# Recurrence gates of a hybrid encoder block as pairs of 64-row matmuls, with r and i brought together by transfers

## The chip, the cores and the metric

The kernel runs on one core of a Trainium2 chip. The metric is the device time of one execution in microseconds (us), as the median of several runs. The profile of a kernel is one execution recorded by the hardware profiler; its engines are PE (matrix multiply; PEld is its weight load), DVE (vector), ACT (scalar and activation functions), POOL and SP (which issue transfers, POOL also small fills).

## The reference

One layer on a sequence of 512 tokens with 1024 features: a half-step SwiGLU feed-forward block, a mixing stage, a second half-step feed-forward block. The mixing stage projects the normalised input to seven groups of 1024 columns; one of them goes through a short convolution and then through two gated linear recurrences, one forward and one backward in time. Their gates are what the change touches: the 1024 features form 16 blocks of 64, and each block has its own 64x64 weight for each direction and each of the two gates r and i.

```python
def _rglru_scan(xc, w_gates, b_gates, lam):
    xb = xc.reshape(B_, S, LRU_BLOCKS, LRU_BLOCK)
    gates = jnp.einsum('bsni,gnio->gbsno', xb, w_gates).reshape(2, B_, S, W)
    gates = gates + b_gates[:, None, None, :]
    r = jax.nn.sigmoid(gates[0])
    i = jax.nn.sigmoid(gates[1])
    log_a = -LRU_C * r * jax.nn.softplus(-lam)
    a = jnp.exp(log_a)
    bx = jnp.sqrt(-jnp.expm1(2.0 * log_a)) * (i * xc)
    _, h = lax.associative_scan(_lin_combine, (a, bx), axis=1)
    return h
```

## The kernel before

Activations lie with features on the 128 partitions and the 512 tokens along the free dimension: a tile `f` is 128 features (two gate blocks of 64) by 512 tokens, and there are eight tiles. Matmuls are float32 in three parts: an operand is split into a high part H (by ACT, line 118) and a low remainder L (by DVE, line 121), and a product is H·H + H·L + L·H (`mm3`, lines 144 to 147).

The stages in order: first feed-forward block (`ffn`, with the Strassen-like `strassen`, line 260); the projection that feeds the recurrence, eight chunks (the loop at line 641, with `conv` after each); the q, k, v projections in two halves (`tok_group`, lines 656 to 670, called t0 and t1); the three gate projections of the merge (`gates`, line 836, called g); the output projection; the second feed-forward block.

Two generators run beside these stages, the "lanes": `lru` (line 583), once for tiles 0 to 3 and once for tiles 4 to 7 (lane 0 and lane 1 below), and `heads` (line 710), the attention. `weave` (line 449) advances a lane by so many `yield` steps after each chunk; RATE (line 59) says how many. This order in the program is a priority: a planner at build time orders the instructions of each engine, starting what is ready by its own estimate of times. `after(i, prev)` (line 199) forces the order of two instructions without a wait.

In `lru`, for each tile and each direction `d`, each gate `g` gets one group of three 128x128x512 matmuls (lines 603 and 604). The weight is 128x128 with the two 64x64 blocks of the tile on its diagonal and zeros elsewhere. A sigmoid on ACT (line 606) takes the result out of PSUM; `ix` is multiplied by the convolution's result (line 611) and tanh of the scaled r is taken (line 613) at once. After the four tiles come the exponentials (618), the square roots (623) and the scans (631, 633), one step of the lane for each. The last result `A[f]` is used at line 856, in stage g.

Buffers: four PSUM banks named `acc` for the projections and four named `aux` for the lanes; 48 SBUF slots of 2 KB per partition (`big`), among which are r, ix and th; four slots of twice that size (`pair`); three raw and four split weight buffers. Transfers: weights on SP's queue; on POOL's queue the eight stores and six loads that shift V (lines 693 and 696) and the sixteen loads of the attention bias (line 706). POOL also zeroes the padding of the convolution's input (lines 569 and 570).

Of the kernel before, what the change touches and what calls it, by code (L numbers as in the profile page):

```python
# [11 lines left out]
AF = mybir.ActivationFunctionType  # L12
ALU = mybir.AluOpType
# [3 lines left out]
P = 128  # L17
T = 512
D = 1024
KT = D // P  # L20
# [3 lines left out]
HD = 64  # L24
# [10 lines left out]
C_BG = 64  # L35
# [17 lines left out]
GB_BATCH = (range(0, 4), range(4, 6), range(6, 7), range(7, 8))  # L53

LRU_F = 4

ATT_LAG = 1, 2

# [9 lines left out]
def block_kernel(ctx: ExitStack, tc, a, out):  # L68
    nc = tc.nc
# [11 lines left out]
    def nm(s):  # L81
        uid[0] += 1
        return f"{s}_{uid[0]}"
# [3 lines left out]
    def big_t(dt=F32, shape=(P, T), n="b"):  # L87
        return big.tile(list(shape), dt, tag="big", bufs=NBIG, name=nm(n))
# [4 lines left out]
    def acc_t():  # L93
        return acc.tile([P, T], F32, tag="acc", name=nm("acc"))

    def aux_t():
        return aux.tile([P, T], F32, tag="aux", name=nm("aux"))


    small = const.tile([P, NSMALL], F32, name="small")  # L100
# [15 lines left out]
    def split(raw, H, L, act=True):  # L116
        if act:
            nc.scalar.activation(H, raw, AF.Copy)  # L118
        else:
            nc.vector.tensor_copy(H, raw)  # L120
        nc.vector.tensor_tensor(L, raw, H.bitcast(F32), ALU.subtract)  # L121
# [3 lines left out]
    def raw_t():  # L125
        return wpool.tile([P, 1024], F32, tag="wraw", bufs=3, name=nm("wraw"))

    def hl_t():
        return (wpool.tile([P, 1024], F32R, tag="wh", bufs=4, name=nm("wh")),
                wpool.tile([P, 1024], F32R, tag="wl", bufs=4, name=nm("wl")))  # L130

    def load_w(src, n, act=True):
        raw = raw_t()
        H, L = hl_t()
        s = slice(0, n)
        ld = nc.sync.dma_start(raw[:, s], src[:, s])
        if nld[0] < 8:
            tc.keep_in_program_order(ld)
        nld[0] += 1
        with tc.high_priority():  # L140
            split(raw[:, s], H[:, s], L[:, s], act)
        return H, L

    def mm3(ps, wh, wl, xh, xl, first, last):
        nc.tensor.matmul(ps, wh, xh, start=first, stop=False)  # L145
        nc.tensor.matmul(ps, wh, xl, start=False, stop=False)  # L146
        nc.tensor.matmul(ps, wl, xh, start=False, stop=last)  # L147
# [48 lines left out]
        nc.scalar.activation(r, ps, AF.Copy)  # L196
        return r, rcol, vx

    def after(i, prev):

        i, prev = getattr(i, "ins", i), getattr(prev, "ins", prev)
        tc.add_manual_dep(i, prev.name, mybir.DependencyInfo(
            mybir.DependencyClass.NoSync, mybir.DependencyReason.DATA), reason="order")


    mark = {}
# [242 lines left out]
    def weave(rate):  # L449
        for ln, n in rate.items():  # L450
            q = lanes[ln]
            due[ln] += n
            while due[ln] >= 1 and q:
                try:
                    next(q[0])
                    due[ln] -= 1
                except StopIteration:
                    q.pop(0)
            if not q:
                due[ln] = 0.0  # L460
# [86 lines left out]
    sp4 = const.tile([P, 16], F32, name="sp4")  # L547
# [17 lines left out]
    xc = [None] * KT  # L565
# [13 lines left out]


    last_act = [None]

    def lru(fs):
        un = []
        cuts = {}

        def cut(f):
            if f in fs:
                cuts[f] = big_t(F32R, n="ch"), big_t(F32R, n="cl")
                split(xc[f], *cuts[f])  # L590

        cut(fs[0])
        for f in fs:
            gH, gL = load_w(a["wgate"][f], T)
            cut(f + 1)
            cH, cL = cuts.pop(f)
            yield
            for d in range(2):
                rt = []
                for g in range(2):  # L600
                    q = d * 2 + g
                    s = slice(q * P, (q + 1) * P)
                    ps = aux_t()
                    mm3(ps, gH[:, s], gL[:, s], cH, cL, True, True)
                    t = big_t(n="gate")
                    i = nc.scalar.activation(t, ps, AF.Sigmoid, bias=small[:, C_BG + f * 4 + q : C_BG + f * 4 + q + 1])
                    if last_act[0] is not None:
                        after(i, last_act[0])
                    rt.append(t)
                r, ix = rt  # L610
                nc.vector.tensor_tensor(ix, ix, xc[f], ALU.mult)
                th = big_t(n="th")
                tanh = nc.scalar.activation(th, r, AF.Tanh, scale=sp4[:, f * 2 + d : f * 2 + d + 1])
                un.append((f, d, r, ix, th))
                yield

        for f, d, r, ix, th in un:
            exp = nc.scalar.activation(r, r, AF.Exp, scale=sn8[:, f * 2 + d : f * 2 + d + 1])
            after(exp, tanh)
            nc.vector.scalar_tensor_tensor(ix, r, 1.0, ix, ALU.add, ALU.mult)  # L620
            yield
        for f, d, av, ix, th in un:
            last_act[0] = nc.scalar.activation(th, th, AF.Sqrt)
            after(last_act[0], exp)
            nc.vector.tensor_tensor(ix, ix, th, ALU.mult)
            yield
        h = None
        for f, d, av, ix, th in un:
            if d == 0:
                h = th  # L630
                nc.vector.tensor_tensor_scan(h, av, ix, 0.0, ALU.mult, ALU.add)
            else:
                nc.vector.tensor_tensor_scan(th[:, ::-1], av[:, ::-1], ix[:, ::-1], 0.0, ALU.mult, ALU.add)
                nc.vector.tensor_tensor(h, h, th, ALU.add)
                A[f] = h
            yield
# [4 lines left out]
    for f in range(KT):  # L641
        ps = acc_t()
# [234 lines left out]
    for m in range(KT):  # L877
        nc.sync.dma_start(xres[m], xd[m])
        ps = acc_t()
# [21 lines left out]
def layouts(inp):  # L901

    f = lambda n: np.asarray(inp[n])
    con = np.ascontiguousarray
    o = {}
    x = f("x")[0].reshape(ROWS, NCB, QC, KT, P)
    o["x"] = con(x.transpose(3, 4, 1, 0, 2)).reshape(KT, P, T)

    def feat(w):
        k, n = w.shape  # L910
        return con(w.reshape(k // P, P, n // P, P).transpose(2, 1, 0, 3)).reshape(n // P, P, k)

# [12 lines left out]
    o["wg3"] = np.concatenate([feat(w[:, c]) for c in (1, 5, 6)], 0)  # L925
    qkv = w[:, 2:5].reshape(4, 2, P, 3, 2, T)
    o["wqkv"] = con(qkv.transpose(3, 4, 0, 2, 1, 5)).reshape(6, 4, P, 2 * T)
    o["wout"] = feat(f("w_out")[0])
    wg = f("lru_w_gates")[0]
    bd = np.zeros((KT, P, 4, P), wg.dtype)  # L930
    for b in range(16):
        s = slice((b % 2) * 64, (b % 2) * 64 + 64)
        bd[b // 2, s, :, s] = wg[:, :, b].reshape(4, 64, 64).transpose(1, 0, 2)
    o["wgate"] = bd.reshape(KT, P, 4 * P)
    col = lambda v: np.asarray(v).reshape(-1, KT, P).transpose(2, 1, 0).reshape(P, -1)
    o["small"] = con(np.concatenate([
        col(f("norm_ffn1")[0]), col(f("norm_mix")[0]), col(f("norm_ffn2")[0]),
        col(f("conv_w")[0]), col(f("conv_b")[0]),
        col(f("lru_b_gates")[0].reshape(4, D)), col(f("lru_lambda")[0]),
        np.tile(f("q_norm")[0], 2)[:, None], np.tile(f("k_norm")[0], 2)[:, None]], 1))  # L940


    rp = f("rel_pos_bias")[0]
    t = np.full((NH, ROWS, QC, 3, 2, ROWS, QC), -1.0e30, rp.dtype)
    for ty, n in enumerate((0, 1, 3)):
        for p in range(QC):
            c = n * QC + QC - 1 - p
            cs = min(max(c - 8, 0), GW - 16)
            for k in range(cs, cs + 16):
                hf, kc = divmod(k - KSTART[n], QC)  # L950
                for r in range(ROWS):

# [21 lines left out]
```

## Time and profile before

| what | us |
|---|---|
| median of 3 runs | 1135.82 |
| lowest and highest | 1135.45, 1135.82 |
| the profiled execution | 1135.38 |
| its span, first to last instruction | 1133.6 |
| PE busy | 1126.1 (99%) |
| DVE busy | 836.4 (74%) |
| ACT busy | 594.5 (52%) |
| POOL busy | 19.2 (2%) |

Rows of instructions read: start, duration, engine, line of the kernel, operation, output tile <- input tiles, shapes, how many. A matmul's row is longer than its share of PE, because matmuls overlap in the array: the distance between the starts of two neighbours is what one costs. In rows of groups, the numbers behind the bar are the busy time and the mean length of one, and behind the second bar the idle time of the engine before them, with what ended it.

### The profile page before, as it was taken

The page shows a single profiled execution, that of the slowest core. Times are in us where ns is not written, and L with a number is a line of the kernel's source. Part 1 is how long each engine was busy: PE and PEld are TensorE (multiplying, and loading weights), DVE is VectorE, ACT ScalarE, POOL GpSimd, SP SyncE. Part 2 cuts the span into 40 slices and gives each one's busy share as a digit, 9 for nine tenths or more (in the row PEclk, how much of TensorE's full clock was granted, in tenths as well). Part 3 has the DMA queues.
Part 4 walks back from the last instruction along what each step waited for, and adds up shares of the span by engine and source line. Part 5 has one row for each costly group of instructions (what it writes and reads, how often), then busy time and mean ns, then how long its engine had stood idle before and what let it go on. Part 6 is the DMA issues. An engine that isn't in the chain of part 4 may idle for free.

```text
span 1133.6 us, 17247 instructions
## 1 busy us (share of the span) xinstructions
PE 1126.1 (99%) x6872; PEld 994.0 (88%) x6872; DVE 836.4 (74%) x1288; ACT 594.5 (52%) x896; POOL 19.2 (2%) x52
## 2 busy tenths in 40 slices
PE   9999999999999999999999999999999999999998
PEld 7899999988888888888788887888999999998886
DVE  7898888884836798797855576758688888894542
ACT  8554544563624595985564254656445545464330
POOL 0000000000000000010110000000000000000000
PEclk9999999999999999999999999999999999999999
DMA  8242333443333342453453333355134333353420
GB/s 266 89 131 79 123 97 108 132 133 103 121 98 107 97 158 81 119 170 93 135 145 103 93 102 87 109 168 186 56 83 123 94 110 114 90 171 94 130 75 38
DMA packets 43553, 130.69 MB, mean 115 GB/s; under 512 B 5968, under 2 KB 8272, under 8 KB 43472
## 3 DMA queue, kind: packets, MB, share of 16 engines
q1 hardware_dynamic: 39600, 119.36, 34.4%
q0 software_dynamic: 3296, 9.97, 2.9%
q8 instruction: 54, 0.88, 0.3%
q10 hardware_dynamic: 576, 0.26, 0.1%
q14 instruction: 27, 0.22, 0.1%
HBM read 121.17 MB, written 8.39 MB: 114 GB/s over the span
## 4 chain that ended last, share of the span: by engine, by line
PE 96%; DVE 3%; ACT 1%; issue 0%; DMA 0%; ACTq 0%; DVEq 0%
PE acc L260 29%; PE acc L146 11%; PE acc L145 11%; PE acc L147 11%; PE aux L260 5%; PE aux L145 4%; PE aux L146 4%; PE aux L147 4%; PE acc L666 3%; PE acc L665 3%; PE acc L667 3%; PE aux L794 1%; DVE wl L121 1%; PE aux L783 1%; DVE so L767 1%; PE aux L757 1%
## 5 line engine op out<-in xcount | busy, mean ns | idle before, releaser
L118 ACT ACTIVATE wh<-wraw 128x1024 fp32r<-128x1024 f32 (+3 forms) x242 | 241.5, 999 | 334.6 <-PE acc L260 96.8
L121 DVE TENSOR_TENSOR wl<-wraw,wh 128x1024 fp32r<-128x1024 f32 (+3 forms) x254 | 291.7, 1151 | 137.6 <-ACT wh L118 136.9
L260 PE MATMUL acc<-s,wh 128*128 128x256 f32 x1216 | 220.6, 283 | 0.1
L260 PEld LDWEIGHTS acc<-s,wh 128*128 128x128 f32 x1216 | 189.7, 192 | 0.3 <-ACT p L317 0.3
L260 PE MATMUL acc<-s,wl 128*128 128x256 f32 x608 | 172.1, 283 | 0.0
L145 PE MATMUL acc<-xh,wh 128*128 128x512 f32 x304 | 120.3, 396 | 0.0
L146 PE MATMUL acc<-xl,wh 128*128 128x512 f32 x304 | 119.5, 393 | 0.0
L147 PE MATMUL acc<-xh,wl 128*128 128x512 f32 x304 | 119.0, 391 | 0.0
L260 PEld LDWEIGHTS acc<-s,wl 128*128 128x128 f32 x608 | 116.7, 192 | 0.0
L260 PE MATMUL acc<-xh,wl 128*128 128x256 f32 x304 | 86.0, 283 | 0.0
L260 PE MATMUL acc<-xl,wh 128*128 128x256 f32 x304 | 86.0, 283 | 0.0
L260 PE MATMUL acc<-xh,wh 128*128 128x256 f32 x304 | 86.0, 283 | 0.0
L665 PE MATMUL acc<-wh,xh 128*128 128x512 f32 x192 | 75.4, 393 | 0.0
L666 PE MATMUL acc<-wh,xl 128*128 128x512 f32 x192 | 74.8, 390 | 0.0
L667 PE MATMUL acc<-wl,xh 128*128 128x512 f32 x192 | 74.8, 389 | 0.0
L294 DVE TENSOR_TENSOR wraw<-wraw,pair 128x1024 f32<-128x1024 f32 x57 | 69.6, 1221 | 0.8
L145 PE MATMUL aux<-hh,wh 128*128 128x512 f32 x176 | 68.5, 389 | 0.0
L146 PE MATMUL aux<-hl,wh 128*128 128x512 f32 x176 | 68.5, 389 | 0.0
L147 PE MATMUL aux<-hh,wl 128*128 128x512 f32 x176 | 68.5, 389 | 0.0
L145 PE MATMUL acc<-hh,wh 128*128 128x512 f32 x176 | 68.5, 389 | 0.0
L146 PE MATMUL acc<-hl,wh 128*128 128x512 f32 x176 | 68.5, 389 | 0.0
L147 PE MATMUL acc<-hh,wl 128*128 128x512 f32 x176 | 68.5, 389 | 0.0
(194 smaller groups left out, 2197.1 us busy)
## 6 DMA issues: line engine op xcount, KB each, us to landing
wraw<-wqkv SPq DMA_DIRECT2D x24, 512.0 KB, 3.7
wraw<-wg SPq DMA_DIRECT2D x24, 512.0 KB, 3.6
wraw<-w1d SPq DMA_DIRECT2D x22, 512.0 KB, 3.6
wraw<-w2d SPq DMA_DIRECT2D x22, 512.0 KB, 3.6
pair<-w2s SPq DMA_DIRECT2D x20, 512.0 KB, 3.6
wraw<-w2s SPq DMA_DIRECT2D x20, 512.0 KB, 3.7
wraw<-w1s SPq DMA_DIRECT2D x18, 512.0 KB, 3.8
pair<-w1s SPq DMA_DIRECT2D x18, 512.0 KB, 3.7
```

Of the source, the lines that this page charges most:

```text
L118: nc.scalar.activation(H, raw, AF.Copy)
L121: nc.vector.tensor_tensor(L, raw, H.bitcast(F32), ALU.subtract)
L145: nc.tensor.matmul(ps, wh, xh, start=first, stop=False)
L146: nc.tensor.matmul(ps, wh, xl, start=False, stop=False)
L147: nc.tensor.matmul(ps, wl, xh, start=False, stop=last)
L260: nc.tensor.matmul(o, w_[:, c], x_, start=first and m + k == 0 and w_ is H and x_ is xh_, stop=m + k == 4 and w_ is L, skip_group_check=True)
L294: nc.vector.tensor_tensor(t, t, o, ALU.add)
L665: nc.tensor.matmul(pss[j], xh[kk][:, tj], H[:, s], start=kk == 0, stop=False)
L666: nc.tensor.matmul(pss[j], xl[kk][:, tj], H[:, s], start=False, stop=False)
L667: nc.tensor.matmul(pss[j], xh[kk][:, tj], L[:, s], start=False, stop=kk == KT - 1)
L757: nc.tensor.matmul(ps[hp][:, i * 256 : (i + 1) * 256], q_[o, n * P : (n + 1) * P], keys(k_[o]), start=k_ is kh and q_ is qh, stop=q_ is ql)
L767: nc.vector.tensor_tensor_reduce(so[:, cs], ps[hp][:, cs], bm[:, BTYPE[n]], -1.0, 3.0e38, ALU.add, ALU.min, nmx[:, i : i + 1])
```

## The change

- The gate weights are stored without zeros: for each tile 128 partitions (two blocks of 64 rows) by 256 columns, which are, for each direction, 64 columns of r and 64 of i.
- For a tile, all four PSUM banks are taken at once. Each direction has three products (H·H, H·L, L·H), and each product is a pair of matmuls with 64 rows, one for the block on partitions 0 to 63 and one for the block on 64 to 127. That is a run of six pairs per tile, held together by `after`. The first of them waits (with a semaphore, `sync=True`) for the last sigmoid of the tile before.
- A result bank now holds r of one block on partitions 0 to 63 and i of the same block on 64 to 127. The sigmoids, four per tile as before, write them to a `pair` buffer, `both`; four transfers on POOL's queue per direction (64 rows of 2 KB each) put the two r halves into `r` and the two i halves into `ix`.
- The product with `xc` and tanh (`use`) move from directly behind the sigmoids to two tiles later (`LRU_LAG`); a lane has five steps more, 41 instead of 36.
- On the host, the layout of the gate weights and of their bias follows.

```diff
+LRU_LAG = 2
...
-    def after(i, prev):
+    def after(i, prev, sync=False):
...
-            mybir.DependencyClass.NoSync, mybir.DependencyReason.DATA), reason="order")
+            mybir.DependencyClass.Sync if sync else mybir.DependencyClass.NoSync, mybir.DependencyReason.DATA), reason="order")
...
+        def use(f, d, r, ix):
+            nc.vector.tensor_tensor(ix, ix, xc[f], ALU.mult)
+            th = big_t(n="th")
+            un.append((f, d, r, ix, th))
+            return nc.scalar.activation(th, r, AF.Tanh, scale=sp4[:, f * 2 + d : f * 2 + d + 1])
...
-            gH, gL = load_w(a["wgate"][f], T)
+            gH, gL = load_w(a["wgate"][f], 2 * P)
             cut(f + 1)
             cH, cL = cuts.pop(f)
             yield
+            ps = [[aux_t() for _ in range(2)] for _ in range(2)]
+            mm = None
             for d in range(2):
-                rt = []
-                for g in range(2):
-                    q = d * 2 + g
-                    s = slice(q * P, (q + 1) * P)
-                    ps = aux_t()
-                    mm3(ps, gH[:, s], gL[:, s], cH, cL, True, True)
-                    t = big_t(n="gate")
-                    i = nc.scalar.activation(t, ps, AF.Sigmoid, bias=small[:, C_BG + f * 4 + q : C_BG + f * 4 + q + 1])
+                c = slice(d * P, (d + 1) * P)
+                for W, X in ((gH, cH), (gH, cL), (gL, cH)):
+                    for b in range(2):
+                        o = slice(b * HD, (b + 1) * HD)
+                        prev, mm = mm, nc.tensor.matmul(
+                            ps[d][b], W[o, c], X[o], start=W is gH and X is cH, stop=W is gL)
+                        if prev is not None:
+                            after(mm, prev)
+                        elif evicted:
+                            after(mm, evicted[-1], True)
+            for d in range(2):
+                q = C_BG + f * 4 + d * 2
+                both = pair_t()
+                for b in range(2):
+                    i = nc.scalar.activation(both[:, b], ps[d][b], AF.Sigmoid, bias=small[:, q + b : q + b + 1])
                     if last_act[0] is not None:
                         after(i, last_act[0])
-                    rt.append(t)
-                r, ix = rt
-                nc.vector.tensor_tensor(ix, ix, xc[f], ALU.mult)
-                th = big_t(n="th")
-                tanh = nc.scalar.activation(th, r, AF.Tanh, scale=sp4[:, f * 2 + d : f * 2 + d + 1])
-                un.append((f, d, r, ix, th))
-                yield
+                evicted.append(i)
+                r, ix = (big_t(n="gate") for _ in range(2))
+                for g, t in enumerate((r, ix)):
+                    for b in range(2):
+                        nc.gpsimd.dma_start(t[b * HD : (b + 1) * HD], both[g * HD : (g + 1) * HD, b])
+                got.append((f, d, r, ix))
+            yield
+            while len(got) > 2 * LRU_LAG:
+                tanh = use(*got.pop(0))
+            yield
+        for _ in range(LRU_LAG):
+            yield
+            yield
+            for t in got[:2]:
+                tanh = use(*t)
+            got = got[2:]
+        yield
...
-    o["wgate"] = bd.reshape(KT, P, 4 * P)
+    o["wgate"] = con(wg.reshape(2, 2, KT, 2, 64, 64).transpose(2, 3, 4, 0, 1, 5)).reshape(KT, P, 4 * 64)
```

More of the change, by code (lines that the diff above doesn't have):

```diff
@@ L581, in block_kernel @@
     last_act = [None]
+    evicted = []
     def lru(fs):
         un = []
+        got = []
         cuts = {}
+        def use(f, d, r, ix):
[3 more added lines that the diff above has]
+            return nc.scalar.activation(th, r, AF.Tanh, scale=sp4[:, f * 2 + d : f * 2 + d + 1])
         def cut(f):
@@ L929, in layouts @@
     wg = f("lru_w_gates")[0]
[L930 to L933, printed above, removed]
-    o["wgate"] = bd.reshape(KT, P, 4 * P)
+    o["wgate"] = con(wg.reshape(2, 2, KT, 2, 64, 64).transpose(2, 3, 4, 0, 1, 5)).reshape(KT, P, 4 * 64)
     col = lambda v: np.asarray(v).reshape(-1, KT, P).transpose(2, 1, 0).reshape(P, -1)
+    bg = f("lru_b_gates")[0].reshape(2, 2, KT, 2, 64).transpose(1, 4, 2, 0, 3).reshape(P, 4 * KT)
     o["small"] = con(np.concatenate([
@@ L938, in layouts @@
         col(f("conv_w")[0]), col(f("conv_b")[0]),
-        col(f("lru_b_gates")[0].reshape(4, D)), col(f("lru_lambda")[0]),
+        bg, col(f("lru_lambda")[0]),
         np.tile(f("q_norm")[0], 2)[:, None], np.tile(f("k_norm")[0], 2)[:, None]], 1))
```

## The prediction

> **What bounds the kernel now.** I read the page first, its busy times and its chain.
>
> ```profile
> span 1133.6 us, 17247 instructions
> PE 1126.1 (99%) x6872; PEld 994.0 (88%) x6872; DVE 836.4 (74%) x1288; ACT 594.5 (52%) x896; POOL 19.2 (2%) x52
> PE 96%; DVE 3%; ACT 1%; issue 0%; DMA 0%; ACTq 0%; DVEq 0%
> ```
>
> PE carries 96% of the chain that ends last. A busy PE need not be a PE at its peak, so the next view is the timeline of PE at one tile's gates, where what counts is the step from one start to the next, not the length of a row.
>
> ```profile
> 389.87 0.39 PE L147 MATMUL acc<-xh,wl 128*128 128x512 f32 x1
> 390.09 0.39 PE L145 MATMUL aux<-ch,wh 128*128 128x512 f32 x1
> 390.32 0.39 PE L146 MATMUL aux<-cl,wh 128*128 128x512 f32 x1
> ...
> 392.59 0.39 PE L147 MATMUL aux<-ch,wl 128*128 128x512 f32 x1
> 392.81 0.39 PE L145 MATMUL acc<-xh,wh 128*128 128x512 f32 x1
> ```
>
> From 390.09 to 392.81 PE starts this tile's twelve gate matmuls and nothing else: 2.72 us, 0.227 us each, the same as its neighbours. There is no idle to win; the only way to shorten this stage is to give PE less. The question is then whether the other engines can follow. The same stretch by windows, columns as in its first row:
>
> ```profile
> core 0: us, PE busy (x) PEld busy (x) DVE busy (x) ACT busy (x) POOL busy (x), PEclk, DMA share, GB/s
> 400.00:410.00 10.00, 10.00 (x46) 8.25 (x45) 9.26 (x12) 10.00 (x15) 0.92 (x2) 1.00 0.87 295
> 410.00:420.00 10.00, 10.00 (x45) 8.28 (x45) 9.62 (x14) 9.94 (x14) 0.00 (x0) 1.00 0.33 101
> 440.00:450.00 10.00, 10.00 (x46) 8.28 (x45) 6.76 (x12) 2.64 (x4) 0.00 (x0) 1.00 0.26 79
> 480.00:490.00 10.00, 10.00 (x46) 8.29 (x45) 9.12 (x14) 9.97 (x15) 2.27 (x4) 1.00 0.64 189
> ```
>
> ACT is full at 400 to 420 and at 480 to 490, yet PE loses nothing there; between the two bursts ACT has room (2.64 of 10). The waits say why:
>
> ```profile
> ACT wh L118 <- PE acc L666: 33.7, 11, 4.8
> PE aux L783 <- DVE nmx L767: 0.8, 2, 0.6
>   PEld aux L145: 0.4, 1
> ```
>
> The first row (all waits): the weight splits of the q, k, v projections wait 33.7 us for PE to free a buffer, so the splits are ahead of PE. The second is the longest wait of PE itself after the start; the third, from the gates' own tile view, is the only one PE had on a gate sigmoid, 0.4 us.
>
> **The change part by part.**
>
> *Fewer matmul steps.* The gate matmuls between 380 and 490 us, by line:
>
> ```profile
> L145 PE MATMUL aux<-ch,wh 128*128 128x512 f32 x32 | 12.2, 397 | 0.0
> L146 PE MATMUL aux<-cl,wh 128*128 128x512 f32 x32 | 12.5, 389 | 0.0
> L147 PE MATMUL aux<-ch,wl 128*128 128x512 f32 x32 | 12.5, 389 | 0.0
> ```
>
> 96 matmuls at 0.227 us are 21.8 us. Half of each 128x128 weight is zeros. The change makes them 96 matmuls with 64 rows, in pairs on rows 0 to 63 and 64 to 127, each pair with its two results in two banks. The trace has that form already, in the attention scores:
>
> ```profile
> 524.30 0.39 PE L667 MATMUL acc<-wl,xh 128*128 128x512 f32 x1
> 524.62 0.38 PE L757 MATMUL aux<-kh,qh 64*128 64x256 f32 x2
> 524.85 0.28 PE L757 MATMUL aux<-kl,qh 64*128 64x256 f32 x2
> 524.97 0.28 PE L757 MATMUL aux<-kh,ql 64*128 64x256 f32 x2
> ...
> 525.32 0.29 PE L757 MATMUL aux<-kh,ql 64*128 64x256 f32 x2
> 525.54 0.66 PE L731 MATMUL aux<-ident,qk 128*128 128x128 f32 x4
> ...
> 526.39 0.48 PE L665 MATMUL acc<-wh,xh 128*128 128x512 f32 x1
> 526.70 0.39 PE L666 MATMUL acc<-wh,xl 128*128 128x512 f32 x1
> ```
>
> Each row is a pair, and pairs follow at 0.12 us for 256 columns: half of the 0.227 that 512 columns take, for two matmuls. So a pair costs what one matmul costs; for 512 columns I take 0.227. 48 pairs are 10.9 us: 10.9 us less.
>
> *Going in and out of 64 rows.* The same rows price it. Into the run: 524.30 to 524.62 is 0.32 where 0.23 is usual (+0.09); the first pair to the second is 0.23 instead of 0.12 (+0.11); out: 525.32 to 525.54, 0.22 instead of 0.12 (+0.10); the first full matmul back, 526.39 to 526.70, 0.31 instead of 0.23 (+0.08, though transposes lie between). Together 0.38 us a run, 0.30 without the last. One run per tile, eight tiles: 3.0 us (2.4 to 3.0). If a run is broken up by other matmuls, each break costs 0.38 more.
>
> *One joint wait per tile.* A tile now takes all four banks of `aux` at once, and its first matmul waits for the last of the four sigmoids of the tile before. Queued behind it on PE is everything. Before, the banks were taken one by one under the same condition, at 0.4 us in all, because other matmuls were put in between. I take 0.1 us for seven waits, 0.7 us, between zero and, if PE stood while two sigmoids of 0.69 us (below) ended, 1.4 each, 9.7 us; nearer to the row of 0.4.
>
> *ACT and DVE.* Sigmoids (32), tanh (16) and products (16) keep number and size; the split of the gate weights halves from 512 to 256 columns, eight times, 0.3 us less on each engine. Nothing on PE's path, because splits are ahead.
>
> *Sixty-four transfers on POOL's queue*, four per tile and direction, 64 rows of 2 KB. Nearest rows, of the V transfers (128 rows of 2 KB) and the bias loads:
>
> ```profile
> L693 POOL DMA_DIRECT2D vd<-v x8: 596/630/771, 483.4 to 568.5; - x8
> DMA to landing us min/median/max: 4.1/4.7/5.0
> 398.64 2.29 POOL L706 DMA_DIRECT2D bm<-rpb  x4 [0.44 <-issue]
> 398.06 0.10 POOL L569 MEMSET xp<- 128x2 f32 x1 [11.02 <-DVE xc L577]
> 410.37 0.82 ACT L575 ACTIVATE xc<-xp,small 128x512 f32<-128x512 f32 x1
> ```
>
> Issue is 0.57 to 0.63 us each, so 8 x 0.6 = 4.8 us per tile, 38 us in all on an engine that works 19.2. They overlap in flight (four loads issued in 2.29 us). The last of a tile lands about 4.8 + 4.7 = 9.5 us after its first issue. Against that stand the starts of the first and the fourth tile of each lane:
>
> ```profile
> 384.06 1.21 PE L145 MATMUL aux<-ch,wh 128*128 128x512 f32 x4
> 401.22 0.39 PE L145 MATMUL aux<-ch,wh 128*128 128x512 f32 x1
> 452.90 0.39 PE L145 MATMUL aux<-ch,wh 128*128 128x512 f32 x1
> 477.38 0.39 PE L145 MATMUL aux<-ch,wh 128*128 128x512 f32 x1
> ```
>
> That is 17.2 / 3 = 5.7 us a tile in lane 0 and 24.5 / 3 = 8.2 in lane 1; with 1 us less of PE work, 4.7 and 7.2. Two tiles later is 9.4 and 14.4 us: just covered in lane 0, well covered in lane 1. I cost it at nothing. What stands behind them on POOL: the padding memsets (the last at 398.06, used at 410.37, 12 us of cover), the bias loads and the V transfers, wanted by attention only. The transfers' 8.4 MB ride beside a DMA share of 0.87 at its worst; if this cover goes, tanh waits at the head of ACT.
>
> *The chain ends later.* Five more steps of each lane before its exponentials. The gates' own view:
>
> ```profile
> L606 ACT ACTIVATE gate<-aux,small x32: 667/686/721, 385.8 to 481.7; 128x512 f32<-128x512 f32 x32
> L633 DVE TENSOR_TENSOR_SCAN th<-gate,gate x8: 1199/1216/1221, 428.8 to 512.0; 128x512 f32<-128x512 f32 x8
> 601.63 1.89 DVE L856 TENSOR_TENSOR A<-pair,th 128x512 f32<-128x512 f32 x3
> ```
>
> The last backward scan starts near 512 and the first result is multiplied at 601.6. Ten us later costs nothing there.
>
> *Sum.* The profiled execution is 1135.38 us (span 1133.6), 0.4 below the median 1135.82. 1135.4 - 10.9 + 3.0 + 0.7 = 1128.2 us. All of it is on PE, and PE is the chain.
>
> [...] Between 400 and 420 us, where the transfers go out, DVE is 93 to 96% busy; the rows of V were issued at 480 to 490 beside a DVE at 91% and took no longer than the rest. [...]
>
> **The rivals.**
> - *Slower: transfers miss their use.* Tanh of tile f stands at the head of ACT until its transfers land; behind it are sigmoids (PE's banks), the q and k evictions and splits. It decides when a tile's eight issues take longer than a tile's period, 4.8 against 4.7 us in lane 0. At 1.2 us an issue (twice the row) a tile takes 9.6, four tiles slip 4 x 4.9 = 20 us, 10 beyond the two tiles' lag, and with the landing's 4.7 ACT stands 15 us. The splits are ahead by the longest wait above, 4.8, so 10 reach PE: 1138. No gain is left from 7.2 + 4.8 = 12 us of standing ACT, an issue near 1.05 us. Against: 0.63 is the median, 0.77 the worst. [...]
> - *Tiles run out.* `big` has 48 slots. When the q and k results of the second half are evicted (503.4 in the ACT timeline below), lane 1 holds 24 (r, ix, th for 8), A holds 4, q and k of the first half 8, V 7: 43, and the eviction wants 5. Before, the scans had begun to free them; ten us later they have not. If they are missed, PE stands until one or two scans of 1.2 us and their neighbours end, 2 to 5 us: 1130 to 1133.
>
> ```profile
> 503.42 0.60 ACT L678 ACTIVATE qk<-acc 128x512 f32<-128x512 f32 x1 [0.52 <-PE acc L667]
> ```
>
> - *It does not pair at 512 columns*, or the waits pull runs apart: 21.8 us again plus 3.0, or half the gain at eight extra breaks (3.0): 1138 or 1131. The rows of 256 columns speak against the first.
> - *No change:* joint waits of about 1 us each, 7 us: 1135.
>
> **How the numbers follow.** Forecast with its own range 1126 to 1130 (free switches at the last step, waits at zero, or waits of 0.3 us): 0.62. Slots or broken runs, 1130 to 1133: 0.18. Joint waits eat it, about 1135: 0.09. Late transfers, 1138: 0.08; no pairing, 1138: 0.03. A difference of 0.2% (2.3 us) is about what can be told from none; so faster 0.80, within 0.09, slower 0.11. The range 1126 to 1134 leaves out the last three.
>
> **What would show it.** Right: in the gates' rows on PE, x2 with 64 rows, 0.227 us from pair to pair, six pairs together, about 1.7 us a tile; PE still gapless between; POOL issues near 0.6 us; tanh with no wait for a DMA. Wrong: PE waits on gate sigmoids over 0.3 us, ACT waits of th on DMA, a qk eviction that waits for a scan, or pair steps of 0.45 us.

## The result, and the profile after

| | before | after |
|---|---|---|
| median of 4 runs, us | 1135.73 | 1147.39 |
| lowest, highest | 1135.45, 1135.82 | 1146.83, 1149.29 |
| profiled span | 1133.6 | 1145.9 |

The kernel became slower: ratio 1.0108, 95% interval 1.0096 to 1.012, where 1128.2 us was forecast. From the page of the kernel after: its span, the granted clock of PE in 40 slices, and two rows on transfers. Under it stand the same two rows from the page of the kernel before:

```profile
span 1145.9 us, 17428 instructions
PEclk9999999999999999989999999999999999999999
q0 software_dynamic: 6368, 18.36, 5.6%
wraw<-wqkv SPq DMA_DIRECT2D x24, 512.0 KB, 5.6
```
```profile
q0 software_dynamic: 3296, 9.97, 2.9%
wraw<-wqkv SPq DMA_DIRECT2D x24, 512.0 KB, 3.7
```

POOL's queue (q0) moves 8.4 MB more, and the weight loads of the q, k, v projections, which have nothing to do with the gates, take 5.6 us from issue to landing instead of 3.7.

Line numbers from here on are those of the kernel after: 123 the low remainder of an operand split on DVE; 592 the product and 595 tanh; 617 the pairs; 627 the sigmoids; 635 the gates' transfers; 650 the exponentials; 697 to 699 the q, k, v matmuls and 710 their q, k eviction (the copy out of PSUM); 725 and 728 V's stores and loads; 770 and 772 the low remainders of q and k (ql, kl) and 815 a transpose in the attention. In some kernels of the experiments they are shifted by a few lines.

**The pairs do what was forecast.** One run of PE's timeline:

```profile
389.80 0.39 PE L149 MATMUL acc<-xh,wl 128*128 128x512 f32 x1
390.12 0.50 PE L617 MATMUL aux<-ch,wh 64*128 64x512 f32 x2
390.46 0.40 PE L617 MATMUL aux<-cl,wh 64*128 64x512 f32 x2
390.69 0.40 PE L617 MATMUL aux<-ch,wl 64*128 64x512 f32 x2
...
391.38 0.40 PE L617 MATMUL aux<-ch,wl 64*128 64x512 f32 x2
391.72 0.50 PE L147 MATMUL acc<-xh,wh 128*128 128x512 f32 x1
392.05 0.39 PE L148 MATMUL acc<-xl,wh 128*128 128x512 f32 x1
```

Pairs follow at 0.23 us; going in, the first pair, going out and the first matmul back are about 0.10 us longer than 0.23 each, 0.4 us a run. Two of the eight runs are broken up: other matmuls follow their first pair (at 384.01 and at 402.93), so PE goes into 64 rows ten times.

**What PE lost instead.** PE's waits between 380 and 580 us (us in total, times, longest), and the waits of the other engines on the gates' transfers:

```profile
PE acc L697 <- ACT qk L710: 5.2, 1, 5.2
PE aux L815 <- DVE ql L770: 4.2, 1, 4.2
PE aux L617 <- DVE cl L123: 1.7, 1, 1.7
PE aux L617 <- ACT pair L627: 0.6, 1, 0.6
```
```profile
DVE gate L592 <- DMA gate<-pair: 29.8, 9, 11.8
ACT th L595 <- DMA gate<-pair: 9.9, 1, 9.9
```

PE stands 11.7 us. The product (L592) waits 29.8 us at the head of DVE: it is DVE's next instruction, and all that stands behind it waits too. Tanh waits 9.9 us at the head of ACT. The first stop comes about so: DVE waits 4.24 us for a gate transfer until 394.81, splits a weight behind the product, comes to cl only at 396.56, and PE, which needs cl, stands 1.7 us. Three windows (busy time of each engine, granted clock, DMA share) show what comes with each stop:

```profile
398.40:401.80 3.40, 3.40 (x11) 2.39 (x8) 2.96 (x5) 3.40 (x6) 2.96 (x6) 0.50 1.03 293
507.60:514.40 6.80, 4.50 (x11) 3.53 (x12) 6.05 (x11) 6.80 (x12) 0.00 (x0) 0.50 0.40 131
541.80:548.50 6.70, 5.93 (x18) 4.64 (x19) 6.63 (x18) 4.25 (x11) 0.58 (x1) 0.50 0.28 79
```

The granted clock falls to 0.50 for 3.4 or 6.8 us; within them matmuls of 512 columns follow at 0.43 us instead of 0.23. As an estimate, half of PE's busy time there is lost: (3.40 + 4.50 + 5.93) / 2 = 6.9 us. Together 11.7 + 6.9 - 6.5 (the pairs, by the span of pairs_alone below, 1127.1) = 12.1 us, against 12.3 between the spans of after and before; as pairs_alone has a wait of 0.7 us of its own in its span, this agrees to about 1 us and no better. Ahead of the first fall, at 398.4, PE had stood 0.6 and 1.7 us, with half a microsecond of work between.

**The longest stop, step by step.** POOL's, DVE's, ACT's and PE's timelines around 480 to 511 us:

```profile
480.20 2.08 POOL L635 DMA_DIRECT2D gate<-pair  x4 [2.21 <-ACT pair L627]
482.27 2.45 POOL L725 DMA_DIRECT2D vd<-v  x4
490.85 0.60 POOL L728 DMA_DIRECT2D vs<-vd  x1 [6.13 <-DMA vd<-v]
...
495.02 2.64 POOL L635 DMA_DIRECT2D gate<-pair  x5
500.18 1.06 POOL L635 DMA_DIRECT2D gate<-pair  x2 [2.52 <-DMA vs<-vd]
501.46 0.52 POOL L635 DMA_DIRECT2D gate<-pair  x1 [0.22 <-DMA gate<-pair]
```
```profile
502.38 0.69 DVE L592 TENSOR_TENSOR gate<-gate,xc 128x512 f32<-128x512 f32 x1 [11.83 <-DMA gate<-pair]
```
```profile
501.65 0.73 ACT L595 ACTIVATE th<-gate,sp 128x512 f32<-128x512 f32 x1 [9.91 <-DMA gate<-pair]
...
509.28 0.57 ACT L710 ACTIVATE qk<-acc 128x512 f32<-128x512 f32 x1
```
```profile
509.90 0.79 PE L697 MATMUL acc<-wh,xh 128*128 128x512 f32 x1 [5.16 <-ACT qk L710]
510.49 0.63 PE L698 MATMUL acc<-wh,xl 128*128 128x512 f32 x1
```

The last tile's eight transfers stand on POOL behind four V stores and three V loads, and the first V load waits 6.1 us for its store. They go out from 495 to 502. DVE stands still for 11.83 us and ACT for 9.91 us; then ACT has tanh, the exponentials and splits to do before it comes to the q, k eviction at 509.28, for which PE has stood 5.16 us. The second matmul behind the stop follows at 0.59 us, not 0.23.

**Transfers slow each other.** Windows of after follow; the last but one number is the DMA share. Before, it was 0.87, 0.33 and 0.64 in these three windows.

```profile
400.00:410.00 10.00, 10.00 (x44) 7.22 (x43) 8.19 (x12) 7.30 (x12) 6.63 (x14) 0.91 1.03 284
410.00:420.00 10.00, 10.00 (x46) 8.29 (x45) 7.79 (x11) 7.45 (x12) 3.80 (x9) 1.00 1.04 294
480.00:490.00 10.00, 10.00 (x50) 7.76 (x49) 7.25 (x10) 7.43 (x12) 4.51 (x8) 1.00 1.00 281
```

The DMA engines are full there, by shares of 1.00 to 1.04. The gates' transfers, by issue time in ns (least, median, most) and time to landing:

```profile
L635 POOL DMA_DIRECT2D gate<-pair x64: 518/518/692, 387.4 to 501.5; - x64
...
DMA to landing us min/median/max: 2.4/5.2/8.6
```

The view of transfers for 480 to 500 us (how many, KB each, median us from issue to landing), after and then before:

```profile
wraw<-wqkv SPq DMA_DIRECT2D x4, 512.0 KB, 7.6
gate<-pair POOLq DMA_DIRECT2D x9, 128.0 KB, 5.5
vd<-v POOLq DMA_DIRECT2D x4, 256.0 KB, 8.1
```
```profile
wraw<-wqkv SPq DMA_DIRECT2D x4, 512.0 KB, 3.7
vd<-v POOLq DMA_DIRECT2D x4, 256.0 KB, 4.9
```

### The profile page after: what moved, and what is told of

Read it like the earlier page. It is cut to its first block, busy times and chain, and to the rows that moved or that the text cites. A ratio compares the mean times of both kernels' runs of the same rounds, so it can differ in the third digit from the quotient of the medians.

```text
span 1145.9 us, 17428 instructions
## 1 busy us (share of the span) xinstructions
PE 1126.7 (98%) x6872; PEld 989.1 (86%) x6872; DVE 833.1 (73%) x1288; ACT 589.3 (51%) x894; POOL 52.5 (5%) x116
## 4 chain that ended last, share of the span: by engine, by line
PE 90%; DVE 3%; issue 2%; DMA 2%; POOL 1%; ACT 1%; POOLq 0%; ACTq 0%; DVEq 0%
PE acc L262 29%; PE acc L148 11%; PE acc L149 10%; PE acc L147 10%; PE aux L262 5%; PE aux L148 3%; PE aux L149 3%; PE aux L147 3%; PE acc L697 2%; PE acc L698 2%; PE acc L699 2%; PE aux L826 1%; POOL gate L635 1%; PE aux L815 1%; DVE wl L123 1%
## 5 line engine op out<-in xcount | busy, mean ns | idle before, releaser
L697 PE MATMUL acc<-wh,xh 128*128 128x512 f32 x192 | 77.7, 405 | 5.2 <-ACT qk L710 5.2
```

The lines of the kernel that those rows point to most:

```text
L697: nc.tensor.matmul(pss[j], xh[kk][:, tj], H[:, s], start=kk == 0, stop=False)
```

## The experiments

Theory: the pairs gain what was forecast, and the transfers take it back twice, by filling the DMA engines and by making DVE and ACT wait. Rivals: the later chain, the order on POOL's queue, the issuing queue, the bytes. In the table, the intervals are those of the ratio to the kernel before, whose median beside these kernels was 1135.4 to 1135.7. Not every kernel computes the block: pairs_alone, pairs_lag_no_transfers, transfers_unread and transfers_apart leave out bringing r and i together, and the two half_bytes kernels leave out half of the columns.

| kernel | median us | ratio, 95% interval |
|---|---|---|
| pairs_alone | 1129.13 | 0.9943 [0.9928, 0.9958] |
| pairs_lag_no_transfers | 1130.66 | 0.9956 [0.9939, 0.9972] |
| transfers_apart | 1138.43 | 1.0025 [1.0015, 1.0034] |
| transfers_unread | 1146.86 | 1.0099 [1.0083, 1.0116] |
| transfers_alone | 1148.93 | 1.0117 [1.0102, 1.0132] |
| v_behind | 1144.03 | 1.0074 [1.0059, 1.0089] |
| half_bytes | 1141.02 | 1.0047 [1.0032, 1.0062] |
| half_bytes_v_behind | 1139.75 | 1.0035 [1.0022, 1.0048] |
| act_queue | 1172.66 | 1.0327 [1.031, 1.0344] |
| half_sigmoids | 1150.79 | 1.0135 [1.012, 1.015] |
| halves_dve_copy | 1145.10 | 1.0082 [1.0067, 1.0097] |
| halves_pool_copy | 1142.08 | 1.0057 [1.004, 1.0074] |
| halves_pool_lag1 | 1136.02 | 1.0004 [0.9995, 1.0012] |
| halves_r_transfer_lag2 | 1143.00 | 1.0064 [1.0052, 1.0077] |
| halves_r_transfer_lag1 | 1142.66 | 1.0065 [1.0053, 1.0078] |
| pairs_first_lane | 1134.67 | 0.9994 [0.9985, 1.0002] |
| pairs_second_lane | 1137.52 | 1.0022 [1.0013, 1.0031] |
| pairs_tiles_0_to_2_4_to_6 | 1132.19 | 0.9972 [0.9961, 0.9983] |

### The parts one by one

**pairs_alone**: the sigmoids write r and ix directly; no transfers, no lag.

```diff
-                both = pair_t()
+                r, ix = (big_t(n="gate") for _ in range(2))
-                    i = nc.scalar.activation(both[:, b], ps[d][b], AF.Sigmoid, ...)
+                    i = nc.scalar.activation((r, ix)[b], ps[d][b], AF.Sigmoid, ...)
-                for g, t in enumerate((r, ix)): ... dma_start ...
```

> The pairs and the joint wait, without transfers and without the lag: the sigmoids write straight into r and ix, and tanh and the product follow at once (r and ix then hold mixed halves, so the values are not the block's). Theory 1 (the loss is all in the transfers and what waits for them): 1135.7 - 7.9 + 0.7 = about 1128.5 us, no PE idle over 0.7 us between 380 and 560 us, granted clock 1.00 there. Rival (the joint wait and broken runs on PE cost more than the pairs give): 1135 us or more, PE waits on sigmoids of 1 us each.

It is 6.4 us faster than before, with the clock at 1.00 and one PE wait on a gate sigmoid:

```profile
PE aux L617 <- ACT gate L627: 0.7, 1, 0.7
```

**pairs_lag_no_transfers**: the same, with the product and tanh two tiles later.

> The pairs, the joint wait and the lag of two tiles, but no transfers: the sigmoids write straight into r and ix (mixed halves, so the values are not the block's). It parts the lag from the transfers. Theory 1: the lag alone costs little, 1128 to 1131 us. Rival (five steps more push the scans into the attention's DVE time): an idle of PE near 4 us at the attention's first transposes and its half clock after, 1134 to 1137 us.

This is 1.5 us more than pairs_alone; their intervals overlap, so the lag costs little, if anything. PE waits 0.8 us for ql and 1.3 for a maximum of the scores, where attention meets the later scans.

**transfers_alone**: the 128-row matmuls of before, with transfers and lag.

```diff
-                            ps[d][b], W[o, c], X[o], ...      (pairs)
+                    mm3(ps[d][b], gH[:, s], gL[:, s], cH, cL, True, True)
```

> The 128-row matmuls and the weights of before, no joint wait, but the transfers and the lag of two tiles as in the change. Theory 1: everything that was lost with none of the gain, 1147.4 + 7.9 = about 1155 us (1150 to 1158, less where the slower gates give a transfer more time), with DVE's product and ACT's tanh waiting for transfers and a PE idle of 4 us or more. Rival (the pairs are what stalls PE): about 1136 us.

It is 13 us slower than before without any pair: transfers and lag are enough. Product and tanh wait for the transfers here too (25.2 and 7.3 us). The 1148.9 us are under the 1150 to 1158 expected: the pairs, beside transfers, gain only 1.5 us, and as the intervals overlap, that isn't told from nothing.

**transfers_unread**: pairs and lag as in pairs_lag_no_transfers, and 64 transfers out of r and ix into a buffer that nobody reads.

> Pairs, joint wait and lag, sigmoids straight into r and ix (mixed halves, so the values are not the block's) as in the run without transfers (1130.7 us), and the 64 transfers of the change beside it, of the same sizes and on the same queue, from r and ix into a buffer that nobody reads. It parts what the transfers do by being waited for from what they do to other transfers. Theory H (DVE's product and ACT's tanh stand at the heads of their queues until late transfers land): nobody waits, 1131 to 1133 us, no PE idle over 1.5 us. Theory C (the DMA engines are full in the two bursts and the weight loads come late): the share of the DMA engines stays near 1.0 at 400 to 420 and 480 to 500, weights land in 7 us and PE waits for splits, 1138 us or more.

This doesn't tell the theories apart: the product writes ix in place, so it waits until the transfers out of ix have landed (33.5 us at the head of DVE). The next kernel has no such wait.

**transfers_apart**: the 64 transfers read a constant buffer.

```diff
+    idle = big.tile([P, 2, T], F32, tag="idle", bufs=1, name="idle")
...
+                        after(nc.gpsimd.dma_start(other[b * HD : (b + 1) * HD, g], idle[g * HD : (g + 1) * HD, b]), i, True)
```

> The unread transfers once more, now from a buffer of constants (in the run before, the product overwrote the transfers' source in place and so waited for them all the same): pairs and lag without transfers (1130.7 us), and beside them 64 transfers of 64 rows of 2 KB on POOL's queue, each issued behind its sigmoid, read by nobody and blocking nobody's buffer. The values are not the block's, as r and ix hold mixed halves. Theory H (the loss comes through DVE and ACT standing for these transfers): 1131 to 1134 us. Theory C (it comes through the weight and V transfers that they slow down): 1138 us or more.

No product and no tanh waits for these transfers, and yet it takes 7.8 us more than pairs_lag_no_transfers. Its waits:

```profile
PE aux L816 <- DVE ql L771: 3.6, 1, 3.6
PE acc L698 <- ACT qk L711: 2.9, 1, 2.9
ACT wh L120 <- DMA wraw<-wqkv: 4.0, 2, 3.4
ACT xc L577 <- POOL xp L572: 4.0, 1, 4.0
```

A split waits for its weights, and the convolution for POOL's padding memset, which stands behind the issues; both stand at the head of ACT. The DMA share is 1.04 at 400 to 410. After takes 9.0 us more. As differences of whole kernels that is -6.4 for the pairs, +1.5 for the lag, +7.8 for transfers that nothing of the gates waits for, +9.0 where product and tanh wait for them. The 7.8 isn't all late weights: PE stands until 431 and until 535 here, not until 397, 510 and 542 as in after, and ahead of the first of these stops ACT waits for the memset too, which it doesn't in after. How the 7.8 divides between the full DMA engines and POOL's queue is not settled.

### The order, the bytes, the queue

**v_behind**: V's stores and loads in the order of steps behind the last tile's.

```diff
+        weave(RATE[phase[0]])
         for j in range(NCB):
             nc.gpsimd.dma_start(vd[hf][:, j * QC : (j + 1) * QC, :], V[hf, 2 * j])
...
-        weave(RATE[phase[0]])
```

> The changed kernel with V's four stores and three loads put behind the last tile's eight gate transfers on POOL's queue (they stood ahead of them; the loads wait for the stores to land). Theory 1a (that order makes the late tanh): the wait of 9.9 us on ACT and 11.8 us on DVE at 490 to 502 shrinks below 4 us, the PE idle of 5.3 us at 504 and its 6.8 us of half clock go, 1147.4 - 5.3 - 3 = about 1139 us, less still if the scans, 10 us earlier, leave the attention alone (1133 to 1139). Rival (the transfers are slow by themselves): the waits stay, 1145 to 1148 us.

It gives 3.4 us back, between what the two theories expected. PE's wait for the q, k eviction falls from 5.2 to 2.3 us, but the product still waits 28.3 us in all, and weights come later (their splits wait 5.4 us for them, 1.6 in after). The order is a part, not the whole cause.

**half_bytes**: 256 of 512 columns are moved; DVE fills the rest.

> The changed kernel, but each of the 64 transfers moves 256 of its 512 columns; the other columns of r and ix are set to 0.5 by DVE (so the values are not the block's), 32 short fills. Same number of issues, same queue, same lag. Theory C and every theory in which the transfers are late because the DMA engines are full: landing falls from 5.2 to 4 us or less, and half or more of the loss of 17 us comes back, 1136 to 1141 us. Theory Q (POOL's order and the fixed time from issue to landing make them late): 1144 to 1148 us.

It gives 6.4 us back with the same number of transfers, so the bytes matter; that the number of issues doesn't is not shown, as it was not changed. The landing falls from 5.2 to 4.1 us in the median, but 6.4 of the 17 us that the expectation counts as the loss is less than the half it asked for. One stop remains at the old place: PE waits 6.7 us for the q, k eviction.

**half_bytes_v_behind**: both edits together.

> Both repairs at once: half of the columns transferred (the rest set to 0.5 by DVE, values not the block's) and V's transfers behind the last tile's. Apart they gave back 6.4 and 3.4 us of 17. If the transfers' lateness has these two parts, fullness and order, then 1131 to 1135 us and no PE idle over 3 us near 504. If something else holds the last tile's transfers: 1138 to 1141 us, the idle of 6.9 us stays.

It is only 1.3 us better than half_bytes, and the intervals overlap; tanh of the last tile still waits 6.6 us.

**act_queue**: the 64 transfers are issued from ACT's queue.

```diff
-                        nc.gpsimd.dma_start(...)
+                        nc.scalar.dma_start(...)
```

> The changed kernel with the gate transfers issued from ACT's queue, right behind the sigmoid they wait for; POOL's queue has V and the bias alone, as before the change. Theory Q: the last tile's transfers no longer stand behind V's loads, the 10 us waits at 490 to 502 go, 1134 to 1141 us, with about 64 x 0.33 us (an issue on SP's queue before) = 21 us more on ACT's sequencer. Theory C: the DMA engines are as full as with POOL, 1143 to 1150 us, worse where an issue waits at the head of ACT.

```profile
ACT pair L627 <- DMA gate<-pair: 13.0, 4, 6.3
DVE gate L592 <- DMA gate<-pair: 46.7, 10, 8.3
```

It is 25 us worse than after and well past both ranges; the expectation had said worse only where an issue waits at the head of ACT. ACT's sigmoids now wait 13.0 us at its head for transfers, where they waited 2.1 us in after, and PE stands 9.2 us for them; how the rest of the 25 us comes about was not followed. With the gates' transfers on ACT's queue, the DMA share is still 0.97 and 0.95 at 400 to 410 and 410 to 420 us, and the weights of q, k, v land in 5.0 us instead of 3.7.

### Without transfers, or with few

**half_sigmoids**: four sigmoids of 64 partitions per direction put r and i in place; product and tanh at once.

```diff
+                        i = nc.scalar.activation(
+                            t[b * HD : (b + 1) * HD], ps[d][b][g * HD : (g + 1) * HD], AF.Sigmoid, ...)
```

> A version of the pairs without any transfer: ACT brings r and i together itself, by four sigmoids of 64 partitions per direction instead of two of 128, half of them writing to the other 64 partitions than they read; tanh and the product follow at once. All values are the block's. PE as in the pairs alone (1129.1 us); ACT gets 32 sigmoids more at 0.69 us = 22 us in 100 us of the lanes, where it is 82% busy, so in the two bursts it falls behind and the gates' banks come late. If the planner can put other matmuls there: 1129 to 1132 us, better than before. If ACT becomes the bound of the two bursts: up to 1137 us.

A sigmoid of 64 partitions takes 0.68 us, as long as one of 128. ACT was 19.5 us busy in each of three windows of 20 us (400 to 420, 460 to 480, 480 to 500), and PE waited 7.6 us on gate sigmoids. The 32 further instructions on a full ACT cost more than the transfers (1150.8 us against 1147.4).

**halves_dve_copy, halves_pool_copy**: the product is taken in two halves of 64 rows, which brings i to its place, and DVE or POOL copies 64 rows of r. Tanh at once.

```diff
+            nc.vector.tensor_tensor(ix[:HD], X[HD:], xc[f][:HD], ALU.mult)
+            nc.vector.tensor_tensor(ix[HD:], Y[HD:], xc[f][HD:], ALU.mult)
+            nc.gpsimd.tensor_copy(X[HD:], Y[:HD])
```

> A version with no transfers and no lag, all values the block's: the sigmoids write the two mixed tiles X (r and i of the first block) and Y (of the second); DVE's product takes i where it lies, in two instructions of 64 partitions, into a new tile, and a DVE copy of 64 partitions puts r of the second block into X. ACT as in the pairs alone (1129.1 us). DVE gets 16 products (0.68 us) and 16 copies (0.35 to 0.7) more, 16 to 22 us in two bursts in which it is 85 to 93% busy. If that only shifts work into the slack between the bursts: 1130 to 1134 us. If DVE becomes the bound: 1138 us or more.

> [...] DVE gets 11 us more instead of 16 to 22; tanh waits for POOL. 1129.5 to 1133 us if POOL's copies come in time; DVE may be slowed beside them, then up to 1137 us.

Both are slower than before. Tanh waits at the head of ACT for the copy: 18.7 us in 13 waits for DVE, 14.0 for POOL. PE itself waits for gate sigmoids (5.7 and 3.4 us) and for DVE to evict v (4.7 and 5.3 us), so these two kernels don't part the wait at the head of ACT from DVE's further work. The next one takes the first away.

**halves_pool_lag1**: POOL's copy, V behind, and tanh one tile later.

> No transfers: the product is taken in two halves of 64 rows (which brings i to its place) and POOL copies the 64 rows of r, both at once; only tanh comes later, by one tile, and V's transfers stand behind the last tile's copies. If the loss of the unlagged form (1142.1 us, where tanh waited 14.0 us at the head of ACT for POOL's copies) was the waiting at the head of the queue: waits of tanh on POOL under 2 us, PE's waits on gate sigmoids under 1.5 us in all, 1130 to 1134 us, faster than before. If it was the work itself, 16 more products of about 0.6 us on a DVE that is full between 400 and 420 and between 480 and 490 us: PE waits remain for the v, q and k evictions, 1138 to 1142 us.

```profile
ACT th L594 <- POOL gate L634: 4.9, 2, 3.1
PE aux L788 <- DVE kl L771: 2.9, 1, 2.9
PE acc L696 <- DVE xp L574: 1.1, 1, 1.1
```

It is 6 us better than without the lag (V's order moved as well) and within the interval as fast as before the change, between what the two theories expected. PE no longer waits for gate sigmoids; it waits for a DVE that is full from 400 to 420 and from 500 to 520 (9.6 to 10 of 10).

**halves_r_transfer_lag2, halves_r_transfer_lag1**: as above, but r's 64 rows come by one transfer per tile and direction, 16 in place of 64.

> As above, with r's 64 rows moved by one transfer per tile and direction on POOL's queue (16 transfers in place of 64, a quarter of the bytes) and tanh two tiles later; only tanh can wait for them. If full DMA engines and waits for landings are what makes the change slow: the DMA share stays under 0.95 at 400 to 420 and under 0.85 at 480 to 500, tanh waits under 3 us in all for transfers, and by a quarter of the 7.8 us that crowding cost, on top of pairs with the lag (1130.7), 1132 to 1135 us. If DVE's 16 further products decide: 1138 to 1142 us, with no wait for a DMA. If the order on POOL still decides: tanh of the last tile waits over 4 us, 1136 to 1139 us.

> As the one above with tanh one tile later instead of two. A landing takes about 5 us and a tile 5.7 us in lane 0: if the later chain is a cost of its own (1.5 us for two tiles), 0.5 to 1 us less than with two tiles, 1131 to 1134.5 us; if the landing isn't covered by one tile, tanh waits over 5 us in all at the head of ACT and it is 2 to 5 us more than with two tiles.

Both are slower than every theory said. The lag makes no difference (1143.0 and 1142.7). With two tiles of lag, the landing time of these 16 and the last two tanh on ACT's timeline:

```profile
DMA to landing us min/median/max: 2.1/3.0/10.6
```
```profile
493.10 0.72 ACT L594 ACTIVATE th<-gate,sp 128x512 f32<-128x512 f32 x1 [2.03 <-DMA gate<-gate]
498.44 0.72 ACT L594 ACTIVATE th<-gate,sp 128x512 f32<-128x512 f32 x1 [4.61 <-DMA gate<-gate]
```

In the second lane's first three tiles such a transfer takes 2.2 to 4.4 us. Those of the last tile, issued among V's, take 8.0 and 10.6 (the last was issued at 487.71), and the stop comes back: PE waits 6.5 us for q, k evictions, 3.9 of them at this place. The DMA share from 485 to 498 us is 0.94; in halves_pool_lag1, with V's transfers and none of the gates', it is 0.86. So it is mostly V that fills the engines there, and two small transfers among V's come late.

### Pairs where there is room

The form of halves_pool_lag1 in some tiles, the 128-row form of before in the others.

```diff
+            pairs = f < LRU_F        # or f >= LRU_F, or f % LRU_F < 3
```

> halves_pool_lag1's form (pairs, product in halves, POOL's copy of r, tanh one tile later) in the first lane's four tiles, the second lane and V's transfers as before the change. Pairs gave 6.4 us in eight tiles, 3.2 in four. In halves_pool_lag1 PE lost 1.23 + 0.46 us in this lane (xp at 409.8, gates at 403.3). If the loss is where the further DVE work falls on a full DVE, this lane's remains and the second's (0.79, 3.16 and the half clock behind it) goes: 1133.5 to 1135 us, no half clock. If it is the sum of the further work wherever it is done: half of each, 1135.5 to 1136 us.

> The same form in the second lane's four tiles alone, V's transfers behind the last tile's. If the place decides: 1135.6 - 3.2, and PE's waits at 505 and 520 (0.79 + 3.16, with 1.7 of half clock behind them) remain: 1136 to 1138 us, with DVE full between 490 and 520. If the sum of the further work decides: 1135.5 to 1136 us.

> The same form in the first three tiles of each lane, V's transfers as before the change: the last tile's gates, which stand before the exponentials, are as before, and tanh of the third tile follows behind them. 6 x 0.8 = 4.8 us of pairs. If what costs is the last tile's path into the chain of exponentials and scans: 1131 to 1133 us, PE's wait for kl near 520 under 1 us. If DVE's further 12 products cost where they are: 1134 to 1136 us.

First lane: within the first theory's range, its 1.1 us wait for xp as expected, the interval just reaching no change. Second lane: slower, and the time is within the first theory's range, but by luck, as the waits expected near 505 and 520 are not there; PE waits 3.3 us at 482 for DVE to evict v. All tiles but each lane's last: 3.2 us (0.3%) faster than before; of the kernels that leave nothing out, it is the only one whose interval excludes no change on the fast side. Its PE waits:

```profile
PE aux L148 <- DVE cl L123: 1.0, 1, 1.0
PE aux L832 <- DVE nmx L816: 0.6, 1, 0.6
PE acc L714 <- DVE v L738: 0.6, 1, 0.6
```

There is no wait for kl or for q, k evictions, as expected if what costs is the last tile's path: its gates, on which the exponentials wait, are not made later, and 1132.19 us lies in the 1131 to 1133 of that theory. As V stands here as before and in halves_pool_lag1 behind, the difference between these two kernels (3.8 us) isn't settled between the two edits.

## Why the prediction was wrong, step by step

- *Fewer matmul steps, in and out of 64 rows, joint waits:* 10.9 - 3.0 - 0.7 = 7.2 us was forecast, 6.4 measured in pairs_alone. The switch cost 0.4 a run (0.38 forecast) and the waits 0.7; one run was broken up, at 383.88, so that PE changed nine times and not eight. This part was right in mechanism and nearly in size.
- *Sixty-four transfers, "I cost it at nothing":* this is the step that failed, in three ways.
  - Their load on the DMA engines was named ("a DMA share of 0.87 at its worst") and not multiplied out. The row of q0 before gives it: 2.9% of 16 engines over 1133.6 us for 9.97 MB is 53 engine-us per MB; 8.4 MB are 443, or 28 us of all 16 engines. Half of it, 14 us, falls into each of two bursts of 25 and 40 us (387 to 412 and 462 to 502). Before, the share in these stretches was 0.57 and 0.53. As an estimate, 14 us in 25 add 0.55, to 1.12, more than the engines have, and 14 in 40 add 0.35, to 0.88. Measured after: 0.94 and 0.87, and 1.04 at the busiest (410 to 420 us). With nothing of the gates waiting, the transfers cost 7.8 us (transfers_apart).
  - The lead of two tiles was held against issue and landing of a tile by itself. 4.8 + 4.7 is 9.5 us, already more than the 9.4 called just covered. The issue was shorter than assumed, 0.52 us in the median; the landing wasn't: median 5.2, longest 8.6, and with half the bytes 4.1 and 6.2.
  - What stands *behind* the transfers on POOL was looked at, and not what stands *ahead*: V's loads, waiting for V's stores. The last tile's transfers came 10 us after their sigmoids. And the product on DVE, 29.8 us of waits, was not named as waiting; only tanh was. With product and tanh waiting, the loss grows by 9.0 us (transfers_apart to after).
- *The chain ends later, at nothing:* with the lag alone 1.5 us, inside the uncertainty. With late transfers it counts: the scans run into attention, PE waits 4.2 us for ql.
- *Rival "transfers miss their use":* the right direction and the right place, ACT's head, at the wrong price. It was tied to longer issues, 1.2 us for 1138 and about 1.05 for no gain; in after the issue stayed at 0.52, 0.69 at most. A busy DVE is not what made the longest stop: DVE did nothing from 490.55 to 502.38, and still the five gates' transfers issued from 495.0 to 497.1 us took 5.5 to 6.4 us to land. That its 10 us on PE are near the 11.7 that PE stood is luck: only the 5.2 us for the q, k eviction came by the way it names. What its 1138 left out is the half clock at each stop, 6.9 us as an estimate, and DVE's waits.
- *Rival "tiles run out":* PE did wait for a q, k eviction, but ACT worked without a gap from 501.65 to it, on what the late transfers had held up; no slot was missed there.

## What to carry to other kernels

Before a transfer is costed at nothing, multiply its bytes by the trace's own engine time per byte and add that to the DMA share of the windows where it runs; here, at sums of 1.12 and 0.88 over a burst, everybody's transfers were late, the weights' too (5.6 us in the median, 3.7 before). Read the issuing queue for what stands ahead as well as behind, and ask of every use whether it stands at the head of an engine that others need. A saving on a gapless matmul engine is worth its own size only as long as nothing stops it: here each stop of 1.7 to 5.2 us came with 3.4 or 6.8 us at a granted clock of 0.50.

## What was unexpected of the hardware

- The granted clock fell to 0.50 at 398.4, 1.1 us behind the end of a stop of 1.7 us, and at 507.6 and 541.8, while PE still stood, 2.9 and 3.4 us into the stops of 5.2 and 4.2, in stretches of 3.4 or 6.8 us; before the change no wait of PE behind its start was over 1.1 us, and the mean clock was 1.000. The length of a stop alone doesn't decide it: in halves_dve_copy PE stood 1.9 us for a q, k eviction between 420 and 440, and the clock was 1.00 from 400 to 460. In act_queue the stops brought the mean clock to 0.986.
- From 480 to 500 us, at a DMA share of 0.91 to 1.00, a 512 KB weight load takes 7.6 us; before, at 0.64 to 0.67, it took 3.7. A 128 KB transfer inside SBUF took 2.1 us at its fastest and 10.6 at its slowest in halves_r_transfer_lag2, 2.4 and 8.6 in after.
- A gate's issue on POOL waited 2.52 us at 500.18 for the landing of a V load that it doesn't use. It is the sixth of the last tile's gates, and the first V load stands eight places before it in the queue. Why it waited for that load no run shows.
